# A transformer block's MLP on one core: tokens as the stationary operand of the products, in place of the weights

## The chip, the core and the metric

The kernel runs on one core of a Trainium2 chip. The metric is the device time of one execution in microseconds. Runs of the same kernel lie within some 0.1% of each other; three runs of the kernel before are shown below. One more execution was recorded by the hardware profiler; all durations of single instructions come from it.

## The reference: what is computed

256 tokens and 16 meta tokens (272 rows of 2048 channels) go through one block: a mixer of two attention branches with gates, then an MLP of width 8192 with squared ReLU, each behind an RMS norm and added to the residual h. The change touches the MLP and the norm ahead of it:

```
def rmsnorm(x, g):
    xf = x.astype(jnp.float32)
    y = xf * lax.rsqrt(jnp.mean(xf * xf, axis=-1, keepdims=True) + EPS)
    return (y * g.astype(jnp.float32)).astype(x.dtype)

def squared_relu_mlp(xn, w1, w2):
    return jnp.square(jax.nn.relu(xn @ w1)) @ w2
...
        h = h + squared_relu_mlp(rmsnorm(h, norm_mlp_g[l]), w_ff1[l], w_ff2[l])
    return rmsnorm(h, final_norm_g)[:, N_META:]
```

w_ff1 is 2048 x 8192, w_ff2 8192 x 2048, all in float32. From the MLP on only the 256 tokens are kept.

## The kernel before

**Layout.** Everything is held with channels on the 128 partitions and tokens along the free dimension: h is 128 x 16 (channel blocks) x 272. A product with a weight matrix is made block of 128 output columns by block: `w_all` in DRAM holds 128 x 2048 for one such block (16 k of 128 x 128). `stream()` sets the order of the blocks: 104 for the mixer's input and gates with their projections, 16 for its output, then four groups (g) of 16 blocks of the MLP's first product (ff1, loop f) and 16 of its second (ff2, loop j).

**Precision.** A float32 value is split in two parts that TensorE takes in one pass each (fp32r): hi, the rounded value, and lo, the rest. A product is made of hi·hi + hi·lo + lo·hi. For the activations the parts lie side by side, so that `x[:, k]` is 512 wide: 256 tokens hi, 256 tokens lo.

**Weights.** `next_weights` brings one block in two halves of 8 k. For each half SP issues one load of 512 KB into `raw` (L124; 5 buffers), ACT casts it to hi (L126), DVE takes the difference into lo (L127); both lie in `w` (5 buffers). ACT's cast waits for TensorE to be done with the buffer of five halves before.

**Products.** `gemm2` makes one output block in one PSUM bank: for each k, `mac2` gives two products with the weights stationary and the tokens moving, hi on the 512-wide row (L149) and lo on the 256-wide hi part (L150). `steps` only changes the order in which the columns are walked. The results of the halves of the bank are then added: `total` (L187 on ACT, L190 on DVE) for ff1, `add_residual` (L872 on ACT, L873 and L874 on DVE) into h for ff2.

**The norm between.** `add_residual` after the mixer gives h; `x2` is h with the norm's gain, split in hi and lo (L879, L880); POOL sums the squares in `acc2`. `norm2` splits that sum and multiplies it with a 128 x 128 tile of ones, which gives the sum over the channels on all partitions (`root_of_sums`, L226 and L227), and DVE takes the root. The factor `r2b` (128 x 256) is applied behind the first product, in `relu2` (L893), since it is positive and the same for all channels. `relu2` squares and splits the result into `a` (L194, L195), the moving operand of ff2.

**The end.** In the last group the last four blocks of ff2 are taken apart: lo first for all (L927), then hi for one half of the tokens after the other (L943), so that the final norm and the stores of the first half lie beside the products of the second.

**What sets the order.** Each engine works its instructions in the order of its queue. A scheduler sets that order from a simulated time as the program is built; it decides where ACT's and DVE's work on results stands between the casts of weights. The tile framework sets the waits. POOL's DMAs go through a queue of their own.

**Offsets.** The tiles w, x2, a and whi begin some elements into their buffers (`at=`, and `pair`'s 24), which sets the positions of the operands to each other modulo 64 elements.

Of the kernel before, what the change touches and what calls it, by code (L numbers as in the profile page):

```python
# [7 lines left out]
F32 = mybir.dt.float32  # L8
# [8 lines left out]
P = 128  # L17
# [48 lines left out]
def trunk(ctx: ExitStack, tc: tile.TileContext, hT, w_small, w_all, consts, w_alpha2, out):  # L66
# [3 lines left out]
    def nm(s):  # L70
        serial[0] += 1
        return f"{s}_{serial[0]}"
# [11 lines left out]
    def bank(pool, s):  # L84
        return pool.tile([P, 512], F32, tag="bank", name=nm(s))
# [4 lines left out]
    def later(n, fn):  # L90
        waiting.append([n, fn])
# [13 lines left out]
    chunk = [0]  # L105
    HK = KT // 2

    def pair(meta=False):
        n = HK * P
        w = wp.tile([P, 2 * n + 64], F32R, tag="w", name=nm("w"))  # L110
        a, b = (0, 20) if meta else (24, 24)
        return [w[:, at : at + n].rearrange("p (k m) -> p k m", m=P) for at in (a, n + b)]

    def weight_half(c, i, hi=None, meta=False):

        raw = wp.tile([P, HK * P], F32, tag="raw", name=nm("raw"), bufs=RAW)
        upper, lo = pair(meta)
        if hi is None:
            hi = upper

        def step(k0, n):
            k = slice(k0, k0 + n)
            cols = slice(k0 * P, (k0 + n) * P)
            nc.sync.dma_start(raw[:, cols], w_all[c][:, i * HK * P + cols.start : i * HK * P + cols.stop])  # L124
            r = raw.rearrange("p (k m) -> p k m", m=P)[:, k, :]
            nc.scalar.copy(hi[:, k, :], r)  # L126
            nc.vector.tensor_tensor(lo[:, k, :], r, hi[:, k, :].bitcast(F32), op=ALU.subtract)  # L127

        return hi, lo, step

    def next_weights(keep_hi=None, meta=False):
        c = chunk[0]
        chunk[0] += 1
        parts = []
        for i in range(2):
            hi, lo, step = weight_half(c, i, None if keep_hi is None else keep_hi[:, HK * i : HK * (i + 1), :], meta)
# [84 lines left out]
    def root_of_sums(y, ps, part, v, scale):  # L221


        hi, lo = halves(y.shape[-1])
        split_to(hi, lo, part)
        nc.tensor.matmul(ps, ones_r[:, 0:P], hi, start=True, stop=False)  # L226
        nc.tensor.matmul(ps, ones_r[:, 0:P], lo, start=False, stop=True)  # L227
        r = part
# [648 lines left out]
    for j in range(KT):  # L877
        add_residual(j, gemm2(next_weights(), y))
        nc.scalar.activation(x2[:, j, 0, :], ht[:, j, :], AF.Identity, scale=gain(1, j))  # L879
        nc.vector.scalar_tensor_tensor(x2[:, j, 1, :], ht[:, j, :], gain(1, j),  # L880
                                       x2[:, j, 0, :].bitcast(F32), op0=ALU.mult, op1=ALU.subtract)
        square_sum(j, acc2)
    r2b = keep.tile([P, NT], F32, tag="rb", name="r2b")

    def norm2():
        root_of_sums(r2b, bank(px, "pn")[:, 0:NT], acc2, gat.tile([P, NT], F32, tag="n2", name="n2", bufs=1), 1.0 / D)

    later(1, norm2)


    def relu2(a, f, ps):
        t = total(ps)
        nc.vector.scalar_tensor_tensor(t, t, 0.0, r2b, op0=ALU.max, op1=ALU.mult)  # L893
        s = gat.tile([P, NT], F32, tag="asq", name=nm("asq"))
        nc.vector.tensor_tensor(s, t, t, op=ALU.mult)
        split_to(a[:, f, 0, :], a[:, f, 1, :], s)

    acc = gat.tile([P, NT], F32, tag="acc", name="acc3", bufs=1)
    for g in range(NG):
        a = operand(keep, "a", at=16, tag="s1")  # L900
        held = []
        for f in range(KT):
            ps = gemm2(next_weights(), x2, pool=px if g == 0 and f < 3 else pg)
            if g == 0 and f == 0:
                held.append(ps)
                continue
            if g == 0 and f == 1:
                relu2(a, 0, held.pop())
            relu2(a, f, ps)
        last = g == NG - 1  # L910
        for j in range(KT - NL if last else KT):
            add_residual(j, gemm2(next_weights(), a))
            if last:
                square_sum(j, acc)
                nc.scalar.activation(ht[:, j, :], ht[:, j, :], AF.Identity, scale=gain(2, j))
                if j == 0:
                    tc.keep_in_program_order(nc.scalar.preload_act_table_set("natural_log_exp_and_others"))


    whi = keep.tile([P, 8 + NL * KT * P + 56], F32R, tag="s2", name="whi_last")[:, 8 : 8 + NL * KT * P].rearrange(  # L920
        "p (n k m) -> p n k m", k=KT, m=P)
    ends = []
    for n in range(NL):
        j, ps = KT - NL + n, bank(pg if n < 3 else px, "ps")
        w = next_weights(whi[:, n])
        for k in range(KT):
            nc.tensor.matmul(steps(ps[:, 0:NT]), w(k)[1], steps(a[:, k, 0, :]), start=(k == 0), stop=(k == KT - 1))  # L927
        nc.vector.tensor_tensor(ht[:, j, :], ps[:, 0:NT], ht[:, j, :], op=ALU.add)
        ends.append((j, w, ps))
# [144 lines left out]
```

## Time and profile before

| what | us |
|---|---|
| median of three runs | 1535.07 |
| lowest, highest run | 1534.62, 1535.66 |
| profiled execution, its own time | 1535.16 |
| its span, first to last instruction | 1533.5 |
| mean granted TensorE clock | 0.998 |
| MLP's products, from the first of ff1 to the last four blocks of ff2 | 839.6 to 1501.2 |

In the tables of busy time by stretches a row has the stretch in us, its length, then for PE (matmul), PEld (weight load), DVE, ACT and POOL the busy time with the count of instructions, the granted clock as a share of full speed, the DMA engines' busy share and the GB/s moved. In an order of time a row has the start, the busy time, the engine, the line of the kernel, the tiles written and read, the shape and a count; matmuls are pipelined, so their busy times overlap and their starts tell the pace. A row of waits has who waited for whom, the sum in us, how often, and the longest. A row of DMA issues has the count, the KB of one and the median us from issue to landing.

### The profile page before, as it was taken

Reading aid. Unit: us, or ns where it says so; the run is one execution under the profiler, and the core shown is the slowest. Engines: PE = TensorE matmul, PEld = TensorE weight load, DVE = VectorE, ACT = ScalarE, POOL = GpSimd, SP = SyncE. Lnnn points to the kernel's source line nnn. Section 1 sums busy time; section 2 is a strip of 40 time slices with the busy share of each in tenths; the row PEclk is TensorE's granted clock in tenths of the full one; section 3 lists DMA queues with packets and bytes.
Section 4 is the critical chain, followed back from the end, with each engine's and each line's share of the span. In section 5 each row is a group of like instructions: output and inputs, shape, how many; then the busy total and the mean of one; then the engine's idle time right before and its main releaser. Section 6 shows DMA issues by size and latency. Waiting matters only on the chain.

```text
span 1533.5 us, 25353 instructions
## 1 busy us (share of the span) xinstructions
PE 1522.3 (99%) x9812; PEld 1399.9 (91%) x9812; DVE 1072.2 (70%) x1659; ACT 794.4 (52%) x1271; POOL 130.2 (8%) x213
## 2 busy tenths in 40 slices
PE   9999999999999999999999999999999999999997
PEld 8999999999999999999999999999999999999997
DVE  7898858586666666666787876667766776667665
ACT  7766444555555544544666544445444454444563
POOL 6012010111100000000011000000000000000012
PEclk9999999999999999999999999999999999999999
DMA  9545555565555565655565566655565556555562
GB/s 320 172 153 176 182 162 188 160 212 170 166 167 188 197 198 197 195 199 199 188 209 195 197 198 197 200 195 195 195 203 197 198 196 199 197 197 200 194 195 96
DMA packets 86600, 293.08 MB, mean 191 GB/s; under 512 B 9112, under 2 KB 16800, under 8 KB 86352
## 3 DMA queue, kind: packets, MB, share of 16 engines
q1 hardware_dynamic: 85872, 289.62, 57.4%
q8 instruction: 77, 1.26, 0.3%
q0 software_dynamic: 176, 1.12, 0.2%
q10 hardware_dynamic: 432, 0.72, 0.1%
q14 instruction: 43, 0.35, 0.1%
HBM read 289.32 MB, written 2.11 MB: 190 GB/s over the span
## 4 chain that ended last, share of the span: by engine, by line
PE 96%; DVE 2%; ACT 1%; issue 1%; DMA 0%; POOL 0%; SPq 0%; POOLq 0%; DVEq 0%; ACTq 0%
PE ps L149 50%; PE ps L150 26%; PE psa L154 5%; PE psa L158 4%; PE psa L156 4%; PE ps L364 1%; PE ps L943 1%; PE ps L366 1%; DVE w L127 1%; PE ps L927 0%; DMA raw<-w_all_dram 0%; PE pa L562 0%; PE po L620 0%; DVE room L434 0%; POOL o L991 0%
## 5 line engine op out<-in xcount | busy, mean ns | idle before, releaser
L127 DVE TENSOR_TENSOR w<-raw,w 128x1024 fp32r<-128x1024 f32 x522 | 644.8, 1235 | 260.5 <-ACT w L126 251.3
L126 ACT CAST w<-raw 128x1024 fp32r<-128x1024 f32 x522 | 547.1, 1048 | 275.2 <-PE ps L150 210.1
L149 PE MATMUL ps<-x,w 128*128 128x512 f32 x1952 | 654.7, 381 | 0.0
L150 PE MATMUL ps<-x,w 128*128 128x256 f32 x1952 | 535.7, 274 | 0.0
L149 PEld LDWEIGHTS ps<-x,w 128*128 128x128 f32 x1952 | 366.5, 188 | 62.4
L150 PEld LDWEIGHTS ps<-x,w 128*128 128x128 f32 x1952 | 366.7, 188 | 0.0
L149 PE MATMUL ps<-a,w 128*128 128x512 f32 x960 | 320.2, 380 | 0.0
L150 PE MATMUL ps<-a,w 128*128 128x256 f32 x960 | 263.3, 274 | 0.0
L149 PEld LDWEIGHTS ps<-a,w 128*128 128x128 f32 x960 | 180.3, 188 | 30.9
L154 PE MATMUL psa<-x,w 128*128 128x272 f32 x640 | 181.9, 285 | 0.0
L150 PEld LDWEIGHTS ps<-a,w 128*128 128x128 f32 x960 | 180.3, 188 | 0.0
L158 PE MATMUL psa<-x,w 128*128 128x272 f32 x640 | 179.8, 282 | 0.0
L156 PE MATMUL psa<-x,w 128*128 128x272 f32 x624 | 176.1, 282 | 0.0
L187 ACT COPY evb<-ps 128x256 f32<-128x256 f32 x160 | 59.4, 371 | 205.1 <-PE ps L150 203.5
L190 DVE TENSOR_TENSOR evt<-ps,evb 128x256 f32<-128x256 f32 x158 | 67.0, 424 | 80.1 <-ACT evb L187 79.7
L154 PEld LDWEIGHTS psa<-x,w 128*128 128x128 f32 x640 | 120.2, 188 | 0.2
L158 PEld LDWEIGHTS psa<-x,w 128*128 128x128 f32 x640 | 120.2, 188 | 0.1
L156 PEld LDWEIGHTS psa<-x,w 128*128 128x128 f32 x624 | 117.6, 188 | 0.0
L868 POOL TENSOR_TENSOR acc<-acc,hsq 128x256 f32<-128x256 f32 x26 | 26.5, 1017 | 737.6 <-ACT hsq L867 737.6
L149 PE MATMUL ps<-og,w 128*128 128x512 f32 x256 | 85.8, 380 | 0.0
L149 PE MATMUL ps<-y,w 128*128 128x512 f32 x256 | 85.4, 380 | 0.0
L872 ACT COPY evb<-ps 128x256 f32<-128x256 f32 x76 | 28.2, 371 | 103.3 <-PE ps L150 102.3
(297 smaller groups left out, 1471.2 us busy)
## 6 DMA issues: line engine op xcount, KB each, us to landing
raw<-w_all_dram SPq DMA_DIRECT2D x537, 512.0 KB, 4.5
raw<-w_all_dram SPq DMA_DIRECT2D x8, 384.0 KB, 6.7
h<-hT_dram SPq DMA_DIRECT2D x8, 275.0 KB, 6.8
negc<-fdram POOLq DMA_DIRECT2D x1, 1088.0 KB, 7.9
out_dram<-o SPq DMA_DIRECT2D x2, 512.0 KB, 2.6
raw<-w_all_dram SPq DMA_DIRECT2D x2, 256.0 KB, 3.7
room<-w_small_dram SPq DMA_DIRECT2D x1, 320.0 KB, 8.1
out_dram<-o ACTq DMA_DIRECT2D x1, 320.0 KB, 3.1
```

What stands on the lines that cost most here:

```text
L126: nc.scalar.copy(hi[:, k, :], r)
L127: nc.vector.tensor_tensor(lo[:, k, :], r, hi[:, k, :].bitcast(F32), op=ALU.subtract)
L149: nc.tensor.matmul(steps(ps), hi, steps(row(x)), start=first, stop=False)
L150: nc.tensor.matmul(steps(ps[:, 0:NT]), lo, steps(x[:, 0, :]), start=False, stop=last)
L154: nc.tensor.matmul(steps(ps[:, X_LO]), hi, steps(x_lo[:, k]), start=first, stop=False, skip_group_check=True)
L156: nc.tensor.matmul(steps(ps[:, 0:NA]), lo, steps(x_hi[:, k]), start=False, stop=last and hi is None, skip_group_check=True)
L158: nc.tensor.matmul(steps(ps[:, 0:NA]), hi, steps(x_hi[:, k]), start=False, stop=last, skip_group_check=True)
L187: nc.scalar.copy(b, ps[:, NT:512])
L190: nc.vector.tensor_tensor(t, ps[:, 0:NT], b, op=ALU.add)
L364: nc.tensor.matmul(steps(ps), hi, steps(row(x[:, k])), start=st, stop=False)
L868: nc.gpsimd.tensor_tensor(acc, acc, sq, op=ALU.add)
L872: nc.scalar.copy(b, ps[:, NT:512])
```

## The change

In three of the four groups, and for 12 of the 16 blocks of ff1 in the last, the operands change places. `token_rows` makes four output blocks at a time in two PSUM banks, one for each half of the tokens: 128 tokens of x2 or a are stationary, and the weights of four blocks, 512 columns, are moving. So a bank holds 128 tokens by 512 outputs. For each k and half of the tokens there are three products: x hi with w hi, x hi with w lo, x lo with w hi. `wide_weights` loads for it two k of four blocks at a time, again 512 KB into `raw`, in runs of 1 KB where they were 4 KB, and casts them into the same `w`.

The results have tokens on the partitions. `hidden` takes the norm's factor as ACT's scale for each partition, squares, and hands the rows to `turn`, which brings them back to channels on the partitions: two DVE transposes within 32 x 32 squares, four DMAs of POOL that write the squares to DRAM, and one that reads them back with the squares in place. ACT and DVE then split them into `a`. For ff2, `gathered` adds the groups' results in SBUF (`rows`), and in the third group turns them and has POOL add them to h.

`norm2` now has the sums of squares stationary and a 512-wide tile of ones moving, four products in place of two, and takes the root on two columns (one for each half of the tokens). For the last group the factor is also written to DRAM and read back on all partitions. It is called inside the first group of four blocks, after the tenth k. The offsets of x2, a and whi change, and the old kind of weights has `low` for the last group.

```diff
+    def wide_weights(c0, q):
+        k0 = 4 * q
+        parts = []
+        for i in range(2):
+            raw = wp.tile([P, HK * P], F32, tag="raw", name=nm("raw"), bufs=RAW)
+            hi, lo = (t.rearrange("p k m -> p (k m)").rearrange("p (k c m) -> p k c m", k=2, m=P) for t in pair())
+            r = raw.rearrange("p (c k m) -> p c k m", k=2, m=P)
+            cols = slice((k0 + 2 * i) * P, (k0 + 2 * i + 2) * P)
+            nc.sync.dma_start(r, w_all[c0 : c0 + 4, :, cols].rearrange("c p (k m) -> p c k m", m=P))
+            r = r.rearrange("p c k m -> p k c m")
+            nc.scalar.copy(hi, r)
+            nc.vector.tensor_tensor(lo, r, hi.bitcast(F32), op=ALU.subtract)
+            parts.append([t.rearrange("p k c m -> p k (c m)") for t in (hi, lo)])
+        return lambda k: tuple(t[:, k % 2, :] for t in parts[k % 4 // 2])
...
-    x2 = operand(keep, "x2", at=56, tag="s2")
+    x2 = operand(keep, "x2", at=24, tag="s2")
...
     def norm2():
-        root_of_sums(r2b, bank(px, "pn")[:, 0:NT], acc2, gat.tile([P, NT], F32, tag="n2", name="n2", bufs=1), 1.0 / D)
-
-    later(1, norm2)
+        hi, lo = parts[:, 0:NT], parts[:, NT:]
+        split_to(hi, lo, acc2)
+        v = gat.tile([P, 2], F32, name="r2v", bufs=1)
+        for t in range(2):
+            ps = bank(pg, "pn")
+            for n, part in enumerate((hi, lo)):
+                nc.tensor.matmul(steps(ps), part[:, P * t : P * t + P], steps(unit), start=(n == 0), stop=(n == 1))
+            nc.vector.tensor_copy(v[:, t : t + 1], ps[:, 0:1])
+        root(r2, v, v, gat.tile([P, 2], F32, name="r2r", bufs=1), 1.0 / D)
+        line = dram.tile([1, NT], F32, name="line")
+        nc.gpsimd.dma_start(line.rearrange("o (t p) -> p (o t)", t=2), r2)
+        nc.gpsimd.dma_start(r2b, line.to_broadcast([P, NT]))
...
+    def token_rows(x, n, between=None):
+        pts = [[bank(px, "pt") for _ in range(2)] for _ in range(n)]
+        for i, q in [(i, q) for i in range(n) for q in range(3)] + [(i, 3) for i in range(n)]:
+            w = wide_weights(chunk[0] + 4 * i, q)
+            for k in range(4 * q, 4 * q + 4):
+                hi, lo = w(k)
+                for t, ps in enumerate(pts[i]):
+                    xh, xl = (x[:, k, o, P * t : P * t + P] for o in range(2))
+                    nc.tensor.matmul(steps(ps), xh, steps(hi), start=(k == 0), stop=False)
+                    nc.tensor.matmul(steps(ps), xh, steps(lo), start=False, stop=False)
+                    nc.tensor.matmul(steps(ps), xl, steps(hi), start=False, stop=(k == KT - 1))
+                if between and k == 9:
+                    between()
...
+    def turn(rows):
+        both = gat.tile([P, KT * P], F32, tag="o", name=nm("turn"))
+        for t, r in enumerate(rows):
+            nc.vector.transpose(both[:, 0:1024].rearrange("p (i t j r) -> p t i j r", i=4, t=2, r=32)[:, t],
+                                r().rearrange("p (j i s) -> p i j s", i=4, s=32))
+        back = both[:, 1024:]
+        there = dram.tile([P, 1024], F32, tag="there", name=nm("there"), bufs=2)
+        for c in range(4):
+            nc.gpsimd.dma_start(there.rearrange("(i s) (c e) -> c s i e", i=4, c=4)[c],
+                                both[32 * c : 32 * c + 32, 0:1024].rearrange("s (i e) -> s i e", i=4))
+        nc.gpsimd.dma_start(back, there)
+        return back.rearrange("p (c t j r) -> p j t c r", c=4, t=2, r=32)
+
+    def hidden(a, b, pt):
+        u = gat.tile([P, 2, 512], F32, tag="u", name=nm("u"), bufs=1)
+        def part(t):
+            nc.scalar.activation(u[:, t, :], pt[t], AF.Relu, scale=r2[:, t : t + 1])
+            nc.scalar.activation(u[:, t, :], u[:, t, :], AF.Square)
+            return u[:, t, :]
+        back = turn([lambda t=t: part(t) for t in range(2)])
+        for t in range(2):
+            hi, lo = (a[:, 4 * b : 4 * b + 4, o, P * t : P * t + P].rearrange("p j (c r) -> p j c r", r=32) for o in range(2))
+            split_to(hi, lo, back[:, :, t])
...
+    def gathered(g, b, pt):
+        rs = [rows[:, t, 512 * b : 512 * b + 512] for t in range(2)]
+        for r, ps in zip(rs, pt):
+            if g == 0:
+                nc.scalar.copy(r, ps)
+            else:
+                nc.vector.tensor_tensor(r, ps, r, op=ALU.add)
+        if g < NG - 2:
+            return
+        back = turn([lambda r=r: r for r in rs])
+        for j in range(4 * b, 4 * b + 4):
+            r = ht[:, j, :].rearrange("p (t c r) -> p t c r", t=2, r=32)
+            nc.gpsimd.tensor_tensor(r, r, back[:, j - 4 * b], op=ALU.add)
...
     for g in range(NG):
-        a = operand(keep, "a", at=16, tag="s1")
-        held = []
-        for f in range(KT):
-            ps = gemm2(next_weights(), x2, pool=px if g == 0 and f < 3 else pg)
...
-            relu2(a, f, ps)
...
-        for j in range(KT - NL if last else KT):
-            add_residual(j, gemm2(next_weights(), a))
...
+        a = operand(keep, "a", at=48, tag="s1")
+        for b in range(3 if g == NG - 1 else 4):
+            hidden(a, b, *token_rows(x2, 1, norm2 if (g, b) == (0, 0) else None))
+        for b0, n in () if g == NG - 1 else ((0, 2), (2, 1), (3, 1)):
+            for b, pt in enumerate(token_rows(a, n), b0):
+                gathered(g, b, pt)
+    for f in range(12, KT):
+        relu2(a, f, gemm2(next_weights(low=True), x2))
+    for j in range(KT - NL):
+        add_residual(j, gemm2(next_weights(low=True), a))
+        normed(j)
```

The built programs show what this does to the queues. First TensorE, at the start of the MLP's first product, before (x is x2, w a half of the weights, ps the bank; "4x32x4" is 512 columns, "4x16x4" is 256; ahead of it stand the mixer's last products from y):

```order
L149 MATMUL ps_9203<-y_8375,w_9199 128x4x32x4
L150 MATMUL ps_9203<-y_8375,w_9199 128x4x16x4
L149 MATMUL ps_9258<-x_1211_8413,w_9249 128x4x32x4
L150 MATMUL ps_9258<-x_1211_8413,w_9249 128x4x16x4
...
L149 MATMUL ps_9258<-x_1211_8413,w_9254 128x4x32x4
L150 MATMUL ps_9258<-x_1211_8413,w_9254 128x4x16x4
```

And now, at the same place, the products of one k and the first of a later half (pt are the two banks, one for each half of the tokens; lines are those of the changed kernel):

```order
L939 MATMUL pt_9253<-w_9256,x_1211_8413 128x4x32x4
L940 MATMUL pt_9253<-w_9256,x_1211_8413 128x4x32x4
L941 MATMUL pt_9253<-w_9256,x_1211_8413 128x4x32x4
L939 MATMUL pt_9254<-w_9256,x_1211_8413 128x4x32x4
L940 MATMUL pt_9254<-w_9256,x_1211_8413 128x4x32x4
L941 MATMUL pt_9254<-w_9256,x_1211_8413 128x4x32x4
...
L939 MATMUL pt_9253<-w_9261,x_1211_8413 128x4x32x4
```

Two products for a k and a block, one wide and one half as wide, have become six wide ones for a k and four blocks; a half of `w` lasts two k in place of eight.

Second, ACT in the first product, before, where the results of the blocks f are worked between the casts of weights (evb and asq are `relu2`'s, a its result; what an instruction waits for stands in brackets, with DMAHW the loads):

```order
L126 CAST w_9482<-raw_9481 128x1024 [waits DMAHW1_49,PE_49]
L187 COPY evb_9415<-ps_9382 128x256 [waits DVE_49,PE_49]
L126 CAST w_9529<-raw_9528 128x1024 [waits DMAHW2_49]
L126 CAST w_9534<-raw_9533 128x1024 [waits DMAHW3_49,PE_49]
L194 CAST a_9247<-asq_9359 128x256 [waits DVE_49]
L187 COPY evb_9467<-ps_9434 128x256 [waits PE_49,Activation_49]
```

And now, from the end of the first group of four blocks (u is the row with Relu and square, turn the tile that comes back; DMASW are POOL's DMAs):

```order
L967 ACTIVATE u_9418<-pt_9253,r_9245 128x512 [waits DMASW1_49,DVE_49,PE_49]
L967 ACTIVATE u_9418<-pt_9254,r_9245 128x512 [waits PE_49]
L152 CAST w_9507<-raw_9506 128x1024 [waits DMAHW4_49,Activation_49]
L968 ACTIVATE u_9418<-u_9418 128x512 [waits Activation_49] x2
L152 CAST w_9512<-raw_9511 128x1024 [waits DMAHW5_49,PE_49]
L152 CAST w_9541<-raw_9540 128x1024 [waits DMAHW6_49,PE_49]
L152 CAST w_9546<-raw_9545 128x1024 [waits DMAHW7_49,PE_49]
L152 CAST w_9595<-raw_9594 128x1024 [waits DMAHW0_49,DVE_49,PE_49]
L152 CAST w_9600<-raw_9599 128x1024 [waits DMAHW1_49,DVE_49,PE_49]
L210 CAST a_9252<-turn_9419 128x4x128 [waits DMASW0_49]
L210 CAST a_9252<-turn_9419 128x4x128
L152 CAST w_9629<-raw_9628 128x1024 [waits DMAHW2_49,DVE_49,PE_49]
```

The cast into `a` waits for a DMA now, and five casts of weights stand between the squares and it. Up to the first of these products the queues of all engines are as before but for one memset on POOL; TensorE's queue is as before again from f = 12 of the last group on.

More of the change, by code (lines that the diff above doesn't have):

```diff
@@ L106, in trunk, with pair, weight_half @@
     HK = KT // 2
-    def pair(meta=False):
+    def pair(meta=False, low=False):
         n = HK * P
         w = wp.tile([P, 2 * n + 64], F32R, tag="w", name=nm("w"))
-        a, b = (0, 20) if meta else (24, 24)
+        a, b = (0, 20) if meta else (56, 56) if low else (24, 24)
         return [w[:, at : at + n].rearrange("p (k m) -> p k m", m=P) for at in (a, n + b)]
-    def weight_half(c, i, hi=None, meta=False):
+    def weight_half(c, i, hi=None, meta=False, low=False):
         raw = wp.tile([P, HK * P], F32, tag="raw", name=nm("raw"), bufs=RAW)
-        upper, lo = pair(meta)
+        upper, lo = pair(meta, low)
         if hi is None:
@@ new lines, in trunk @@
+    rows = gat.tile([P, 2, D], F32, name="rows", bufs=1)
+    def gathered(g, b, pt):
[11 more added lines that the diff above has]
+            nc.gpsimd.tensor_tensor(r, r, back[:, j - 4 * b], op=ALU.add)
@@ L898, in trunk, with normed @@
+    def normed(j):
+        square_sum(j, acc)
+        nc.scalar.activation(ht[:, j, :], ht[:, j, :], AF.Identity, scale=gain(2, j))
+        if j == 0:
+            tc.keep_in_program_order(nc.scalar.preload_act_table_set("natural_log_exp_and_others"))
     acc = gat.tile([P, NT], F32, tag="acc", name="acc3", bufs=1)
     for g in range(NG):
-        a = operand(keep, "a", at=16, tag="s1")
-        held = []
-        for f in range(KT):
-            ps = gemm2(next_weights(), x2, pool=px if g == 0 and f < 3 else pg)
[L904 to L908, printed above, removed]
-            relu2(a, f, ps)
@@ new lines, in trunk @@
+        for b in range(3 if g == NG - 1 else 4):
[8 more added lines that the diff above has]
+        normed(j)
+    whi = keep.tile([P, 8 + NL * KT * P + 56], F32R, tag="s2", name="whi_last")[:, 40 : 40 + NL * KT * P].rearrange(
```

25 lines of the change are left out of this document (13 added, 12 removed).

## The prediction

> **What bounds the kernel now.** I read the page's busy shares first, then the table of busy time by stretches, then the order of time on TensorE in the MLP, then the table of waits.
>
> ```profile
> span 1533.5 us, 25353 instructions
> PE 1522.3 (99%) x9812; PEld 1399.9 (91%) x9812; DVE 1072.2 (70%) x1659; ACT 794.4 (52%) x1271; POOL 130.2 (8%) x213
> 0.00:50.00 50.00, 47.95 (x290) 42.45 (x291) 36.84 (x57) 34.20 (x54) 24.02 (x49) 1.00 0.89 287
> 900.00:1000.00 100.00, 100.00 (x601) 90.34 (x601) 65.58 (x87) 45.66 (x62) 0.00 (x0) 1.00 0.61 198
> 1300.00:1400.00 100.00, 100.00 (x601) 90.34 (x601) 67.27 (x91) 46.18 (x64) 0.00 (x0) 1.00 0.59 197
> ```
>
> TensorE is at work 100.00 of 100 us in the MLP, at a granted clock of 1.00, with 601 products in each 100 us; every other engine has a third of its time free and the DMA engines two fifths. So the MLP lasts as long as its products follow each other, and the question is what one product costs from its start to the next one's start. A busy time (380 ns for a 512-wide one) does not say that, since products overlap; the starts do:
>
> ```profile
> 1000.06 0.27 PE L150 MATMUL ps<-a,w 128*128 128x256 f32 x1
> 1000.17 0.38 PE L149 MATMUL ps<-a,w 128*128 128x512 f32 x1
> ...
> 1009.39 0.27 PE L150 MATMUL ps<-a,w 128*128 128x256 f32 x1
> ```
>
> Between the two L150 rows lie 28 pairs of a 512-wide (L149) and a 256-wide product (L150): 9.33 us / 28 = 333.2 ns a pair. At the other end of the pipeline, ACT's cast of weights waits mostly for TensorE to give a buffer back, and DVE waits for ACT's cast; neither holds TensorE up.
>
> ```profile
> DVE w L127 <- ACT w L126: 251.3, 279, 3.7
> ACT w L126 <- PE ps L150: 210.1, 193, 3.6
> L127 DVE TENSOR_TENSOR w<-raw,w 128x1024 fp32r<-128x1024 f32 x522 | 644.8, 1235 | 260.5 <-ACT w L126 251.3
> L126 ACT CAST w<-raw 128x1024 fp32r<-128x1024 f32 x522 | 547.1, 1048 | 275.2 <-PE ps L150 210.1
> ```
>
> **The products.** Before, four column blocks need for each k four pairs, 8 products and 4 x 768 = 3072 columns. Afterwards they need, for two halves of the tokens, three products of 512: 6 products and again 3072 columns. No column is saved; only two products of eight are, with whatever a product costs beyond its columns. This is done for 15 groups of four blocks in the first product and 12 in the second, 27 x 16 = 432 times, and the order has 864 TensorE rows fewer. So I need the distance of 512-wide products that follow each other, each with a stationary load of its own. The first stage, whose tiles were reloaded for each product too, has such rows:
>
> ```profile
> 16.31 1.52 PE L364 MATMUL ps<-x,w 128*128 128x512 f32 x6
> 17.67 0.29 PE L154 MATMUL ps<-x,w 128*128 128x272 f32 x1
> ...
> 21.12 1.05 PE L364 MATMUL ps<-x,w 128*128 128x512 f32 x4
> 22.00 0.61 PE L366 MATMUL ps<-x,w 128*128 128x256 f32 x4
> ...
> 36.80 1.05 PE L364 MATMUL ps<-x,w 128*128 128x512 f32 x4
> 37.68 0.61 PE L366 MATMUL ps<-x,w 128*128 128x256 f32 x4
> ...
> 1501.17 5.74 PE L927 MATMUL ps<-a,w 128*128 128x256 f32 x48
> 1506.75 1.75 PE L943 MATMUL ps<-a,whi_last 128*128 128x256 f32 x14
> 1508.34 1.09 PE L927 MATMUL ps<-a,w 128*128 128x256 f32 x8
> ```
>
> Four in 0.88 us (21.12 to 22.00, and 36.80 to 37.68) are 220.0 ns each, with the rounding of the stamps 219 to 221. A second way: the pair less a 256-wide product. Fourteen of those at L943 take 1.59 us, 113.6 ns each, which leaves 219.6. I take 220.1 ns. Six are then 1320.6 ns against 4 x 333.2 = 1332.8: 12.2 ns a time, and 432 x 12.2 ns = 5.3 us gained. The break-even lies close: 222.1 ns for one wide product.
>
> Bounds from rows. Low: the 48 products of L927 take 5.58 us, 116.2 each, and 333.2 - 116.2 = 217.0 ns for the wide one; 432 x (1332.8 - 1302.0) = 13.3 us gained. High: the six at 16.31 take 1.36 us, 226.7 ns (weights came late there); 432 x (1360.2 - 1332.8) = 11.8 us lost. What speaks for the high end is that the moving operand now lies in w, which ACT and DVE fill all the time, and that the offsets of x2, a and w to each other are new; no row has w moving. Against it: the 601 products per 100 us are the same for all tensors that are moving now, and the engines' writes to w went on beside them.
>
> By the Trainium skill, TensorE: Matmul & The Clock Gate, section Back-to-back issue gap, an isolated warm product costs its columns at 2.4 GHz and 2.5 ns, 215.8 ns for 512. By it six take 1294.8 ns and, against the pairs as measured, 432 x 38.0 ns = 16.4 us would be gained; the measured 220.0 speaks against that, but both rows come from products mixed with narrower ones.
>
> **The second norm.** L226 and L227 were two 256-wide products:
>
> ```profile
> 848.02 0.39 PE L149 MATMUL ps<-x,w 128*128 128x512 f32 x1
> 848.26 0.28 PE L227 MATMUL pn<-csl,ones 128*128 128x256 f32 x1
> 848.38 0.27 PE L150 MATMUL ps<-x,w 128*128 128x256 f32 x1
> ```
>
> L227 puts 0.12 us between its neighbours, so the two cost 0.24. Now four of 512: 4 x 0.22 = 0.88, or 0.64 us more on the path. They wait for the cast of acc2, which stands on ACT after the sixth wide cast; TensorE reaches them after ten k of 1.32 us, 13 us into the group, so I cost their wait at nothing. Its tiny DVE steps on two columns and two POOL DMAs lie beside six more k (7.9 us); without that cover the first Relu would be some us late, once.
>
> **The turn: the new round trip.** After each of 15 groups ACT takes two Relu and two squares of 512, DVE two 32x32 transposes, POOL issues four writes and one read of 512 KB, then ACT and DVE split the result into a. ACT stands still at that cast of a (L210) until the read has landed; queued behind it are the casts of weights, for which DVE's L153 and then TensorE wait. Rows for its steps:
>
> ```profile
> L632 ACT ACTIVATE so<-po 128x512 f32<-128x512 f32 x8 | 4.9, 616 | 0.0
> L195 DVE TENSOR_TENSOR v0l<-p,v0h 128x512 fp32r<-128x512 f32 x4 | 2.7, 685 | 0.0
> 70.82 0.70 POOL L464 DMA_DIRECT2D fdram<-room  x1 [4.96 <-DVE room L463]
> fdram<-room POOLq DMA_DIRECT2D x1, 8.5 KB, 3.3
> negc<-fdram POOLq DMA_DIRECT2D x1, 1088.0 KB, 7.9
> raw<-w_all_dram SPq DMA_DIRECT2D x537, 512.0 KB, 4.5
> raw<-w_all_dram SPq DMA_DIRECT2D x8, 384.0 KB, 6.7
> ```
>
> Let T be the end of a group's products. A group lasts 16 x 1.32 = 21.1 us, an eighth (one cast of weights) 2.64. Two Relu (1.2), a cast (1.05) and DVE's difference of it (1.24) end at T + 3.5, the squares about then. No row has a DVE transpose; between one pass over 512 (0.69) and one over 1024 elements (1.24) for each, both end at T + 4.9 to 6.0. Four issues of 0.7 make T + 7.7 to 8.8; the last write lands 3.3 to 7.9 later, the read is issued in 0.7 and lands 4.5 to 7.9 after that: T + 16 to T + 25. I take T + 17: the writes are pieces of 128 KB, nearer to the 8.5 KB row, and the read has the size of the raw loads. When must it be there? L210 stands behind five casts, the last of which gets its buffer at T + 13.2, so ACT does wait some 3 us. But the next weights to be cast, the third eighth of the group after next, are used from T + 26.4; two L210 (1.2), the cast and its difference take 3.5. TensorE stalls only for a landing after T + 22.9. So I cost 15 turns at nothing, with 6 us of cover; the four turns of the second products (the third group) are waited for by POOL's adds only.
>
> Who else is waited for: a's last quarter is wanted by the second products after six eighth-pairs, 31 us (a landing at T + 17 is early). PSUM: the two-group call takes four banks of five, and the fourth is one that the last Relu reads, free 15 us before it is wanted. SP's queue only issues raw loads, in runs of 1 KB for 4 KB now; the first stage has such runs at 287 GB/s with 0.89 busy, 322 at full, where 198 are needed and a turn adds 1 MB in 21.1 us (50 GB/s). DVE per group: 8 x 1.24 + 2 x 1.24 + 2 x 0.69 = 13.8 of 21.1 us; ACT 8 x 1.05 + 6 x 0.62 = 12.1. POOL has nothing else queued but the adds on h, before the last group. All else, the tail included, stands in the order as before.
>
> **The sum.** The profiled execution took 1535.16 us, 1.7 outside its span and 0.1 above the median of the runs shown. 1535.2 - 5.3 + 0.6 = **1530.5 us**.
>
> **The rivals.** *Wide products are cheaper alone* than in the pairs, 217.0 ns: 1535.2 - 13.3 + 0.6 = 1522.5 us. For it: L927's 116.2; against: the runs of four. With the 215.8 ns of the Trainium skill (TensorE: Matmul & The Clock Gate, Back-to-back issue gap) it would end at 1519.4. *The moving w costs*: from 222.1 ns on the change loses, at 226.7 it ends at 1535.2 + 11.8 + 0.6 = 1547.6. *The turn is late*: with 7.9 us for the writes and the read, and the slower transposes, it lands at T + 25.2, 2.3 us too late; 15 x 2.3 = 34.5 us, 1565. The point is T + 22.9; POOL's issues under load decide. *The change does save products but not time*: at 221 to 222.1 ns, or with a gain eaten by a few small stalls, 1532 to 1537.
>
> **How the numbers follow.** A measurement of this kernel tells about 0.2% (3.1 us) from no change. Forecast 0.54 (its own range 1528 to 1533; 0.05 of it is a gain under 3.1 us), cheaper products 0.13, nothing 0.08, moving w 0.11, late turn 0.14. Faster: 0.49 + 0.13 = 0.62; same 0.13; slower 0.25. The range takes in the cheaper products and the moving w, 1520 to 1548; outside lies the late turn and little else.
>
> **What would show it.** Right: starts of L939 to L941 rows 220 ns apart, some 454 products in 100 us of the MLP, TensorE busy 100 of 100 there, and L210's idle time on ACT of a few us each without a gap on TensorE. A distance over 222 ns shows the moving w; gaps before L939 released by ACT's w at the third cast behind each L210 show the turn. Wrong altogether: a granted clock under 1.00, or DMA waits of ACT's L152.

## The result, and the profile after

| kernel | median us | lowest to highest | ratio to before, 95% interval |
|---|---|---|---|
| before (8 runs beside the change) | 1535.05 | 1534.62 to 1535.70 | |
| changed (8 runs) | 1541.45 | 1540.31 to 1549.17 | 1.0054, 1.0036 to 1.0071 |

The change makes the kernel 6.4 us slower, where 1530.5 was forecast. The runs also lie further apart than before: 9 us from the lowest to the highest against 1. The profiled execution took 1540.96 us. From the page and from the table of busy time by stretches (columns as before):

```profile
span 1539.2 us, 23426 instructions
PE 1519.9 (99%) x8950; PEld 1365.6 (89%) x8950; DVE 988.6 (64%) x1409; ACT 797.2 (52%) x1201; POOL 201.9 (13%) x327
900.00:1000.00 100.00, 97.12 (x433) 80.56 (x432) 49.37 (x47) 48.16 (x57) 6.04 (x11) 1.00 0.70 224
1300.00:1400.00 100.00, 100.00 (x456) 85.31 (x455) 60.62 (x60) 44.98 (x48) 31.54 (x43) 1.00 0.78 249
```

From 1300 to 1400 us TensorE makes 456 products without an idle moment, at a granted clock of 1.00. A stretch also counts the product or two that reach into it from outside, so this is the forecast pace: 100 us hold 454.5 products of 220 ns, and by the records their starts are 220.0 ns apart. From 900 to 1000 us it makes 433 and stands 2.88 us. So what this run loses in the MLP it loses in the first group, and the table of waits for TensorE from 840 to 1500 us says what held it (engine and line, what it waited for, us in all, times, longest):

```profile
PE pt L940 <- DVE w L153: 2.3, 3, 0.8
PE pt L939 <- ACT w L152: 0.6, 2, 0.3
PE ps L165 <- DVE a L211: 0.6, 1, 0.6
```

Weights came late. The distances from start to start that are over 300 ns add up to 5.46 us above 220 ns each; all lie between 887 and 957 us but 0.7 us at 1442. One of these stalls, in the order of time of ACT, DVE and TensorE:

```profile
884.36 1.14 ACT L210 CAST a<-turn 128x512 fp32r<-128x512 f32 x2 [8.98 <-DMA turn<-there]
885.40 1.99 ACT L152 CAST w<-raw 128x1024 fp32r<-128x1024 f32 x2
886.48 2.36 DVE L153 TENSOR_TENSOR w<-raw,w 128x1024 fp32r<-128x1024 f32 x2 [0.17 <-ACT w L152]
887.76 0.19 PEld L940 LDWEIGHTS pt<-w,x 128*128 128x128 f32 x1 [0.45 <-DVE w L153]
887.76 0.50 PE L940 MATMUL pt<-w,x 128*128 128x512 f32 x1
```

ACT stood 8.98 us for the turn's read; only then could the casts of weights queued behind L210 go on, and TensorE ran dry. Why the read was late stands in POOL's order of time:

```profile
858.52 0.79 POOL L920 DMA_DIRECT2D line<-r  x1 [16.16 <-DVE r L254]
868.57 0.56 POOL L921 DMA_DIRECT2D r2b<-line  x1 [9.25 <-DMA line<-r]
869.12 2.21 POOL L957 DMA_DIRECT2D there<-turn  x4
878.48 0.56 POOL L959 DMA_DIRECT2D turn<-there  x1 [7.15 <-DMA there<-turn]
892.25 2.19 POOL L957 DMA_DIRECT2D there<-turn  x4 [13.22 <-DVE turn L952]
```

The first turn's transposes were done at 865.2 us, but its writes were issued only at 869.1: ahead of them in POOL's queue stood the broadcast of r2b, which waited 9.25 us for the norm's own write of 1 KB to land. The median landings, from the rows of DMA issues (count, KB of one, us from issue to landing):

```profile
there<-turn POOLq DMA_DIRECT2D x76, 128.0 KB, 4.6
turn<-there POOLq DMA_DIRECT2D x19, 512.0 KB, 5.7
r2b<-line POOLq DMA_DIRECT2D x1, 128.0 KB, 6.9
line<-r POOLq DMA_DIRECT2D x1, 1.0 KB, 9.8
```

The rest of the loss is at the very end. The last of POOL's compute starts at 1528.39 us in place of 1527.74, but behind the last store the span goes on for 6.2 us in which no engine and no DMA works; before, the last 2.5 us still held a part of the stores' DMA. First the row of after, then that of before:

```profile
1533.00:1539.20 6.20, 0.00 (x0) 0.00 (x0) 0.00 (x0) 0.00 (x0) 0.00 (x0) 0.50 0.00 0
```

```profile
1531.00:1533.50 2.50, 0.00 (x0) 0.00 (x0) 0.00 (x0) 0.00 (x0) 0.00 (x0) 0.50 0.34 125
```

The views leave out what engines do there: each runs a closing drain, and POOL's took 1.88 us before and 9.81 us after, by its record in the trace. It ended 1.1 us ahead of the span's end, and 4.9 us behind SP's.

### The profile page after: what moved, and what is told of

Read it like the earlier page. It is cut to its first block, busy times and chain, and to the rows that moved or that the text cites. A ratio compares the mean times of both kernels' runs of the same rounds, so it can differ in the third digit from the quotient of the medians.

```text
span 1539.2 us, 23426 instructions
## 1 busy us (share of the span) xinstructions
PE 1519.9 (99%) x8950; PEld 1365.6 (89%) x8950; DVE 988.6 (64%) x1409; ACT 797.2 (52%) x1201; POOL 201.9 (13%) x327
## 4 chain that ended last, share of the span: by engine, by line
PE 85%; DMA 6%; ACT 3%; DVE 3%; issue 2%; POOL 1%; POOLq 0%; SPq 0%; ACTq 0%; DVEq 0%
PE ps L165 24%; PE ps L166 13%; PE pt L940 10%; PE pt L941 10%; PE pt L939 10%; PE psa L170 4%; PE psa L174 4%; PE psa L172 4%; DMA turn<-there 3%; DMA there<-turn 2%; PE ps L383 1%; PE ps L385 1%; DVE w L127 1%; ACT w L152 1%; PE ps L1037 1%
## 5 line engine op out<-in xcount | busy, mean ns | idle before, releaser
L165 PE MATMUL ps<-x,w 128*128 128x512 f32 x992 | 334.4, 382 | 0.0
L166 PE MATMUL ps<-x,w 128*128 128x256 f32 x992 | 272.1, 274 | 0.0
L165 PEld LDWEIGHTS ps<-x,w 128*128 128x128 f32 x992 | 186.2, 188 | 31.7
L166 PEld LDWEIGHTS ps<-x,w 128*128 128x128 f32 x992 | 186.2, 188 | 0.0
L940 PE MATMUL pt<-w,x 128*128 128x512 f32 x480 | 182.8, 381 | 0.8 <-DVE w L153 0.8
L939 PE MATMUL pt<-w,x 128*128 128x512 f32 x480 | 182.7, 381 | 0.3 <-ACT w L152 0.3
L941 PE MATMUL pt<-w,x 128*128 128x512 f32 x480 | 182.6, 380 | 0.0
L940 PE MATMUL pt<-w,a 128*128 128x512 f32 x384 | 146.3, 381 | 1.5 <-DVE w L153 1.5
L939 PE MATMUL pt<-w,a 128*128 128x512 f32 x384 | 146.3, 381 | 0.2 <-ACT w L152 0.2
L941 PE MATMUL pt<-w,a 128*128 128x512 f32 x384 | 146.0, 380 | 0.0
L940 PEld LDWEIGHTS pt<-w,x 128*128 128x128 f32 x480 | 90.1, 188 | 17.2 <-DVE w L153 1.5
L939 PEld LDWEIGHTS pt<-w,x 128*128 128x128 f32 x480 | 90.1, 188 | 16.4 <-ACT w L152 0.7
```

What stands on the lines that cost most here:

```text
L165: nc.tensor.matmul(steps(ps), hi, steps(row(x)), start=first, stop=False)
L166: nc.tensor.matmul(steps(ps[:, 0:NT]), lo, steps(x[:, 0, :]), start=False, stop=last)
L939: nc.tensor.matmul(steps(ps), xh, steps(hi), start=(k == 0), stop=False)
L940: nc.tensor.matmul(steps(ps), xh, steps(lo), start=False, stop=False)
L941: nc.tensor.matmul(steps(ps), xl, steps(hi), start=False, stop=(k == KT - 1))
```

## The experiments

All were timed beside the kernel before on the same chip, which gave medians of 1535.1 to 1535.2 us.

**1. The turn without its round trip.** The trip through DRAM is left out; the transposes and all else stay.

```
-        back = both[:, 1024:]
-        there = dram.tile(...)
-        ... four writes and one read on POOL
+        back = both[:, 0:1024]
```

> The changed kernel without the trip through DRAM: turn hands on the squares as DVE's transposes leave them, so the squares of a 128-column group stand in wrong places and the output isn't the reference's. The theory: the changed products gain 4.9 us by themselves (2592 wide products at 220 ns, the pairs before at 333.2, the norm 0.6 more); what was lost is the trip, by late landings in the first group (about 6 us) and by POOL's closing drain (about 5 us). Then this ends at 1530 us, with no gap on TensorE in the MLP and a drain as short as before. Rival one: the drain has nothing to do with POOL's DMAs of the trip, then 1535. Rival two: the gaps come from the wide loads in runs of 1 KB, then gaps stay and it is above 1535.

Measured: 1529.69 us (1529.26 to 1531.04), ratio 0.9963 (0.9950 to 0.9976).

```profile
900.00:1000.00 100.00, 100.00 (x456) 85.33 (x455) 50.76 (x47) 49.62 (x56) 0.00 (x0) 1.00 0.62 199
```

No stall is left, and every wide product starts 220.0 ns behind the one before it. The products' gain of the forecast is there, 5.5 us against before, and all that the change loses hangs on the round trip. The norm's two DMAs are still at their old place here; without a trip beside them they do not hold TensorE up.

**2. The norm's two DMAs behind the first group, in program order.** They were written into a function called at the end of g = 0.

> The changed kernel with the two POOL DMAs that spread the second norm's factor (written to DRAM, read back) moved from the first group of four blocks to the end of the first of the four groups; they are needed in the last group only. The theory: POOL stood at the second of them until the first had landed (9.8 us), the first turn's writes were queued behind and came 3.6 us late, and the delay went from turn to turn through ACT's queue. Then the gaps at 887 to 956 us go, about 6 us, and it ends near 1535.5, with POOL's closing drain as long as in the changed kernel. Rival: the trip is too long by itself, then the gaps stay and it ends at 1540 to 1541.

Measured: 1546.88 us (1541.63 to 1559.31), ratio 1.0081 (1.0052 to 1.0111). It tests nothing, because the scheduler left the DMAs where they were, as POOL's order of time shows:

```profile
859.12 0.79 POOL L922 DMA_DIRECT2D line<-r  x1 [16.16 <-DVE r L254]
870.10 0.56 POOL L923 DMA_DIRECT2D r2b<-line  x1 [10.18 <-DMA line<-r]
```

So it is the change once more, with the same stalls (5.2 us), yet its time is above both numbers of the expectation. Its MLP shows why:

```profile
1000.00:1100.00 100.00, 100.00 (x449) 83.91 (x448) 52.33 (x49) 50.47 (x58) 8.24 (x15) 1.00 0.73 228
```

TensorE is busy 100.00 us and its clock is 1.00, yet it makes 449 products in place of 456. Their starts lie 225 and 222 ns apart in turn, 223.3 in the mean, from 917 us to the end of the second products, some 2270 of them, which is 7.6 us more. With the stalls, 4.9 us of drain and the 1529.7 of experiment 1 that makes 1547.4, for 1547.8 profiled.

**3. All five DMAs of the turn on SP** (`nc.sync` for `nc.gpsimd` in `turn`).

> The changed kernel with the turn's five DMAs issued by SP in place of POOL. The theory (POOL's queue is what is slow: its landings and its drain): landings of 2 to 4 us as for the other loads and stores of SP, no gap on TensorE after the first trip, POOL's drain as short as before: 1530 to 1531. Rival: the landing is long because the DMA engines are loaded, whoever issues, and SP's loads of weights now stand behind the turn's waits; then gaps of TensorE stay or grow and it ends at 1536 or above, though with a short drain.

Measured: 1532.62 us (1530.11 to 1552.39, 10 runs), ratio 1.0009 (0.9980 to 1.0039). The profiled run, the lowest, has no stall and 220.0 ns throughout. The others spread over 22 us; which of SP's waits or the norm's DMAs does it was open.

**4. The trips alone, in the kernel before:** 19 times four writes and one read of an unused tile on POOL.

> The kernel before with 19 trips added that nobody uses: at the same 19 places of the MLP POOL issues four writes of 128 KB and one read of 512 KB. The theory: POOL's closing drain grows with the software queue's use, from under 2 us to some 9.8, and the end comes 5 us later, 1540, while TensorE stays at 100.00 of 100 us in the MLP. Rival: the drain is long in the changed kernel for another reason (the order of its last POOL work, or its waits), then this stays at 1535.

Measured: 1551.44 us (1550.34 to 1552.37), ratio 1.0104 (1.0089 to 1.0119). The trips wait for no result, so the scheduler put them early and in a crowd, the last one at 926 us:

```profile
850.00:900.00 50.00, 44.79 (x257) 38.82 (x257) 33.95 (x61) 24.84 (x41) 11.71 (x16) 0.98 0.73 234
900.00:1000.00 100.00, 100.00 (x603) 90.33 (x602) 67.09 (x91) 46.48 (x64) 2.65 (x5) 1.00 0.69 227
```

So the time fits neither theory: the last 512-wide product starts 10.8 us later than in the kernel before, which neither forecast. These stalls say little of the change, but the end does: POOL's closing drain took 9.65 us here too, 600 us after its last DMA. So it goes by how much POOL has issued, not by how lately.

**5. The norm's DMAs really behind the first group.** A copy of the factor that reads the first group's last rows makes them wait.

```
+        late = gat.tile([P, 2], F32, name="r2late", bufs=1)
+        nc.vector.scalar_tensor_tensor(late, rows[:, 1, D - 2 : D], 0.0, r2, op0=ALU.mult, op1=ALU.add)
-        nc.gpsimd.dma_start(line.rearrange("o (t p) -> p (o t)", t=2), r2)
+        nc.gpsimd.dma_start(line.rearrange("o (t p) -> p (o t)", t=2), late)
```

> Only the second norm's two DMAs on POOL are issued behind the first group, by a copy of the norm's factor that reads the first group's last rows (in the run before, they had stayed ahead of the first turn). Theory A, the 1 KB and 128 KB DMAs of the norm hold POOL's queue for about 10 us ahead of the first turn, and its lateness is handed from block to block by ScalarE's wait: the first turn's writes are issued within 0.5 us of its last transpose (about 865.5 us in place of 869.1), no start-to-start distance over 300 ns in the first group, all 512-wide products 220 ns apart, and about 1535 us (the version without the trip, 1529.7, and some 5 us of POOL's closing drain). Theory B, the trips' own landings are too long in the first group: the stalls of 5 us stay and the time is 1540 or more. Theory C, the pace of 223 ns comes by itself and not behind a stall: no stalls, but products 223 ns apart in some stretch.

Measured: 1535.38 us (1534.88 to 1537.93), ratio 1.0003 (0.9994 to 1.0013). POOL's order of time and the stretch that had stalls:

```profile
866.35 2.25 POOL L961 DMA_DIRECT2D there<-turn  x4 [23.16 <-DVE turn L956]
872.93 0.57 POOL L963 DMA_DIRECT2D turn<-there  x1 [4.33 <-DMA there<-turn]
```

```profile
900.00:1000.00 100.00, 100.00 (x456) 85.31 (x456) 52.39 (x48) 50.46 (x58) 5.49 (x10) 1.00 0.69 221
```

The writes go out 0.3 us after the transposes (866.1), no distance exceeds 300 ns in the whole MLP, and the products keep 220.0 ns. Theory A held with its number. What remains of 1535.4 against 1530 is the drain, 9.82 us here. Three of the ten runs lie at 1536.8 to 1537.9; no profile shows what they have more.

**6. The turn's writes on SP, its read on POOL**, the norm's DMAs again ahead of the first turn.

> The turn's four writes go to SP, its one read stays on POOL: 23 DMAs on POOL in place of 99. If POOL's closing drain goes by the number of its DMAs, 82 ns each (from 1.88 us with 2, 2.05 us with 4, 9.65 us with 97, 9.81 us with 99), it takes 1.88 + 21 x 0.082 = 3.6 us here and ends ahead of SP's own last step, so that nothing is left of it in the span; if it goes by bytes or by packets (half of the turn's bytes are read), it takes about 5.8 us. SP is held only for the transposes and not for the writes' landing. Theory A (a late first turn behind the norm's DMAs): the writes go out at about 865.5 us, the read waits for POOL's r2b step at 868.6 us at most, no stalls: 1530 us, in all rounds within 2 us. Theory B (SP's waits make the spread of 1530 to 1552 us seen with all five DMAs on SP): some rounds above 1535 us still.

Measured: 1540.37 us (1534.03 to 1552.39), ratio 1.0043 (1.0020 to 1.0067). The drain took 3.60 us, as forecast from the number of DMAs, and ended ahead of SP's last step. The rest of the expectation failed: there were stalls (1.0 us in all), though neither POOL's queue nor SP held the writes (issued at 865.6, right behind the transposes). Their read could be issued only at 875.8, when the last had landed, and the chain of waits shows that loads of weights were caught as well (start, us, what):

```profile
861.15 11.06 DMA raw<-w_all_dram
...
874.64 8.20 DMA raw<-w_all_dram
882.84 0.02 issue
882.86 0.61 ACT a L210
883.47 0.96 ACT w L152
884.43 0.02 issue
884.45 1.24 DVE w L153
885.69 0.04 issue
885.73 0.49 PE pt L940
```

Two loads of 512 KB took 11.06 and 8.20 us, where the median in the kernel before is 4.5. L210 also stands a cast further forward in ACT's queue here (behind four casts from the squares on, not five), as it does in experiment 7.

So the norm's DMAs do not only stand in a queue; what else is in flight around them is late. The traces of experiments 1 and 5 show this apart from the turn. The norm's write of 1 KB is under way from 858.4 to 868.2 us in experiment 1, which makes no trip, and from 1010.9 to 1019.8 in experiment 5. Two stretches, first in experiment 1, then in experiment 5:

```profile
862.00:868.00 6.00, 6.00 (x29) 5.13 (x28) 5.34 (x7) 4.80 (x7) 0.00 (x0) 1.00 0.55 55
1013.00:1019.00 6.00, 6.00 (x29) 5.10 (x29) 3.17 (x3) 2.09 (x2) 0.00 (x0) 1.00 0.75 236
```

```profile
862.00:868.00 6.00, 6.00 (x29) 5.13 (x28) 3.55 (x4) 4.41 (x6) 1.65 (x3) 1.00 0.61 192
1013.00:1019.00 6.00, 6.00 (x29) 5.13 (x28) 2.66 (x3) 2.58 (x3) 0.00 (x0) 1.00 0.45 55
```

Wherever the write is, the core's DMAs move 55 GB/s, and elsewhere 192 and 236. The loads of weights that are issued meanwhile take 8.6 to 11.0 us in the one and 9.3 to 10.7 in the other; in the kernel before, none of the MLP's 247 loads takes over 6.5. The broadcast of r2b can't be the cause, since it is issued only when the write has landed. Why 1 KB does this is not shown; by the records of experiment 1, the write's own packets have all started by 861.3 us.

Most of what this run loses is not in its stalls. Behind the second one, from 929 us to the end of the wide products, 2194 of them keep the slow pace of experiment 2, 223.4 ns, which is 7.4 us:

```profile
1300.00:1400.00 100.00, 100.00 (x450) 83.89 (x448) 57.97 (x58) 43.50 (x47) 18.19 (x21) 1.00 0.78 248
```

**7. Both edits, 5 and 6.**

> Both edits together: writes on SP, read on POOL, the norm's DMAs behind the first group. Theory A: 1530 us in all rounds, no stall, drain 3.6 us, 0.3 percent faster than the kernel before. Theory B (SP's waits for transposes make late weights in some rounds): the same spread as with all five DMAs on SP, 1530 to 1552 us.

Measured: 1530.87 us (1529.90 to 1531.82), ratio 0.9973 (0.9961 to 0.9984). Theory A held; one stall of 0.7 us in the last group was not expected.

**8. All five DMAs on SP, and the norm's behind the first group** (edits 3 and 5).

> All five DMAs of the turn on SP, as in the run that spread from 1530 to 1552 us, and now the norm's two DMAs behind the first group. Theory A, the norm's DMAs collide with the first turn's writes and with the loads of weights that are under way at that time (with the writes on SP a load of weights took 11.06 us from its issue at 861 us, where the median is 4.6, and the first read was issued 10 us behind the writes in place of 5): no spread, 1530 us in all rounds within 2 us, no stall. Theory B, SP's wait for the transposes and for the writes' landing holds the loads of weights: the spread up to 1552 us stays.

Measured: 1530.28 us (1529.74 to 1531.02, 7 runs), ratio 0.9969 (0.9958 to 0.9980). The spread of experiment 3 is gone, so SP's waits did not make it by themselves. This version beats both kernels.

```profile
900.00:1000.00 100.00, 100.00 (x457) 85.30 (x456) 51.37 (x48) 49.06 (x56) 0.00 (x0) 1.00 0.72 228
```

The edits of 5 and 8 differ only in the turn's queue; 1535.38 - 1530.28 = 5.1 us is what the POOL queue costs when it stalls nothing.

**9. and 10. Five pauses of TensorE,** in the version without the trip and in the kernel before: at five loads of weights ACT's copy is repeated 10, 11, 12, 13 and 14 times.

```
-            nc.scalar.copy(hi, r)
+            for _ in range(1 + (more if i == 0 else 0)):
+                nc.scalar.copy(hi, r)
```

> The version without the DRAM trip (1529.7 us, all wide products 220.0 ns apart), and in five of the 108 loads of wide weights ScalarE's copy is repeated 10, 11, 12, 13 and 14 times, which holds TensorE for one pause each (some 1 to 6 us); its output is not the reference's, as the trip is left out. Theory A, the pace that the wide products take up is set by how they resume: behind some of the pauses they run at 223.3 ns (225 and 222 in turn) until the next pause, behind others at 220. Theory B, the slower pace comes from the trips' DMAs: 220 ns behind all five pauses.

Each kernel was run once, for the profile. The first (1575.95 us; the longest distance in each pause is 2.2 to 11.3 us), products of the wide form alone, each row a stretch of 40 us ahead of the first pause and behind each of the five (here the table has no column for POOL):

```profile
900.00:940.00 40.00, 40.00 (x183) 34.15 (x182) 0.00 (x0) 2.70 (x4) 1.00 0.58 191
960.00:1000.00 40.00, 40.00 (x181) 33.56 (x180) 0.00 (x0) 3.51 (x6) 1.00 0.60 195
1080.00:1120.00 40.00, 40.00 (x184) 34.12 (x183) 0.00 (x0) 2.70 (x4) 1.00 0.62 201
1160.00:1200.00 40.00, 40.00 (x184) 34.12 (x183) 1.76 (x3) 0.00 (x0) 1.00 0.61 198
1240.00:1280.00 40.00, 40.00 (x181) 33.55 (x180) 0.00 (x0) 2.71 (x4) 1.00 0.61 198
1360.00:1400.00 40.00, 40.00 (x183) 34.12 (x182) 2.56 (x4) 0.00 (x0) 1.00 0.61 200
```

Behind the first and the fourth pause there are 180 weight loads in 40 us, behind the others 182 or 183; by the records the starts are 223.35 ns apart on the mean in the two, to the next pause, and 220.0 in the three. No trip was there. Theory A held.

> The kernel before with the same five pauses: ScalarE's copy of weights repeated 10 to 14 times at the same five places of its MLP; nothing is left out. Theory A, the slower pace that the wide products took up behind two of five pauses is one of runs of equal products with the tokens stationary: here, where a 512-wide and a 256-wide product alternate, each pair takes 333.2 ns behind all five pauses, as before them. Theory B, any products can resume at a slower pace: pairs of more than 335 ns in one stretch or another.

The kernel before with the pauses (1588.9 us, all products):

```profile
900.00:940.00 40.00, 40.00 (x242) 36.12 (x241) 26.88 (x40) 21.19 (x30) 0.00 (x0) 1.00 0.58 192
960.00:1000.00 40.00, 40.00 (x242) 36.14 (x241) 25.01 (x31) 18.46 (x24) 0.00 (x0) 1.00 0.60 197
1060.00:1100.00 40.00, 40.00 (x237) 35.53 (x236) 30.32 (x48) 20.24 (x31) 0.00 (x0) 1.00 0.61 198
1160.00:1200.00 40.00, 40.00 (x243) 36.12 (x242) 24.94 (x31) 17.68 (x23) 0.00 (x0) 1.00 0.60 199
1260.00:1300.00 40.00, 40.00 (x242) 36.12 (x242) 29.79 (x46) 20.10 (x30) 0.00 (x0) 1.00 0.60 198
```

Behind the second pause a pair takes 340.0 ns, behind the others 333.4. Theory A fell here and B held: pairs can resume slower too. In the profile of the kernel before, where no such pause occurs, they keep 333.3 through the MLP.

## Why the prediction was wrong

**What bounds the kernel: right.** TensorE's order of products still sets the MLP, and whatever starves it is paid in full.

**The products: right in kind and size.** 220.0 ns was measured for 220.1 taken, and the version without the trip is 5.5 us faster than before, for 5.3 - 0.6 = 4.7 forecast. The moving w cost nothing by itself. The rule of 215.8 ns from the Trainium skill (TensorE: Matmul & The Clock Gate, Back-to-back issue gap) is not borne out by these products: each has its own stationary load, and over 2,000 of them in a row kept 220.0.

**The turn: right by itself.** With the norm's DMAs out of the way (experiment 5) the second Relu waits for the end of the group's products at 861.8 us and L210 starts at 878.3, T + 16.5, for T + 17 taken. A transpose took 0.69 us, the lower bound. The point of T + 22.9 held as well: in the change the first read landed at T + 23.4 (884.3 against 860.9) and TensorE lost 0.3 us; the next landed at T + 25.3 (907.4 against 882.1) and cost 1.6.

**The step that failed** is that of the second norm: "Its tiny DVE steps on two columns and two POOL DMAs lie beside six more k (7.9 us); without that cover the first Relu would be some us late, once." The Relu was in time; r2 does not go through the DMAs at all. What the two DMAs hold up is the first turn, by two ways that I did not cost: its writes are queued behind them on POOL, where r2b's broadcast waits for a write of 1 KB that took 9.8 us to land; and the transfers in flight around that write, weights and the turn's writes among them, are late (experiment 6 leaves only this, and stalls remain). Experiment 5 takes both away, and with them all stalls. The first read is issued at T + 17.5 in the change, at T + 14.5 in experiment 6 and at T + 11.2 in experiment 5, so each of the two ways is about half of the delay. I had bounded the turn's landings by POOL's rows of 8.5 KB and 1088 KB, but not the norm's. The Trainium skill's fit for DMAs from GpSimd (DMA: Bandwidth & Descriptors, Anatomy of one DMA) makes it, as an estimate, 2.0 us for 1 KB; here it was 8.9 to 10.7 in the nine profiles that have it.

Nor was it "once". The late L210 delays the casts of weights and also the next two Relu, which stand behind it on ACT; so the next turn starts late, and its L210 with it. The lateness is handed on at about 23 us a block in place of 21.1 until the second products, which have no L210. That is the mechanism of the rival "the turn is late", with another cause and in 4 of 15 turns.

**The second step that failed:** "All else, the tail included, stands in the order as before." The order does, but POOL's closing drain grows with the number of DMAs that POOL has issued. From the records of the trace:

```
DMAs issued on POOL             2     4    23    97    99
packets of that queue         176   256  2992  6560  6640
closing drain, ns            1881  2053  3601  9648  9813
```

(9813 - 1881) / 97 = 82 ns a DMA, and 1881 + 21 x 82 = 3603 fits the third column; by packets it would be 5300. Up to about 5 us it lies beside the last stores; the rest is paid, 4.9 us here by the records and 5.1 by experiments 5 and 8.

**A third part was not thought of:** one price was taken for a wide product, though what pace it resumes at after a stall is open. In the profiled run of the change the three stretches between the first group's stalls, 280 products in all, ran at 222.7 to 224.1 ns, some 0.9 us.

The sum with these: 1530.5 + 5.5 + 4.9 + 0.9 = 1541.8, for 1541.0 profiled; with the 1529.7 of experiment 1 in place of the forecast it is 1541.0. That the higher runs of the change, up to 1549, kept the slow pace through the MLP, as the profiles of experiments 2 and 6 did, fits (2592 products x 3.3 ns = 8.6 us) but was not seen, since only one run of each kernel is profiled. 1552 us, as in experiments 3 and 6, needs more than that; in experiment 6 some 95 products behind the first stall lay 222 to 233 ns apart, 228.5 in the mean, and a run that stayed there would have it. Not tested.

## What to carry to other kernels

A transfer that nobody waits for can still cost: ask what is queued behind each DMA's wait on its issuing engine and what else is in flight, above all for a tiny one like the norm's write here; if its result is needed late, tie it to something late, since moving it in the program alone does not move it when a scheduler sets the order. Count the DMAs that a change puts on GpSimd, some 82 ns each at the closing drain, and put plain copies on SP if its queue can bear the waits, as it did in experiment 8; the Trainium skill (DMA: Bandwidth & Descriptors, SWDGE vs HWDGE vs iDMA) also gives plain transfers to SP or ACT, and experiment 8 agrees with it (1530.3 us, for 1535.4 with the turn on POOL). And a stall in a kernel bound by TensorE may cost more than its own length, since the products behind it can run on at a slower pace: 1.0 us of stalls and 7.4 us of pace in experiment 6.

## What the runs showed of the hardware that I had not expected

- At a granted clock of 1.00, 512-wide products with a load each run 220.0 ns apart, or 225 and 222 in turn (223.3), and mostly keep the pace they resumed with until the next pause: in two of five pauses the slow one. (One stretch of experiment 6 went from 228.5 to 220.0 at 907 us with no pause between.) Pairs of 512 and 256 have 333.3 and 340.0, the slow one behind one pause of five. What decides it was not found.
- POOL's closing drain: 1.88 us with 2 DMAs, 9.81 with 99, whether the last was issued 100 or 600 us earlier.
- A DMA of 1 KB from POOL, two elements of each partition that lie apart in DRAM, landed after 8.9 to 10.7 us, later than 512 KB from POOL (5.7), and while it was under way the core's DMAs moved 55 to 62 GB/s (six us of each of the nine profiles that have it) where the kernel before has 192, and loads of 512 KB took up to 12.1 us.
